# Three waiting projection matmuls placed between the four transposes of an attention output

## The chip, the cores and the metric

One core of one Trainium2 chip runs the kernel. The time is device microseconds from one launch to its end. TensorE is PE in the profile (its weight loads are PEld), VectorE is DVE, ScalarE is ACT, GpSimd is POOL, and SyncE, which issues the DMAs, is SP.

## The reference

The kernel computes one encoder layer on 1024 tokens of width 1024 with two kinds of attention side by side.

```
h = x @ w_in                                   # (1024, 3328): q_a k_a v_a z_a q_b k_b v_b z_b
y_a = neighborhood_attention(q_a, k_a, v_a, rel_bias)     # 8 heads, window 8 x 16 on a 16 x 64 grid
y_b = windowed_gqa_with_sink(rotary(q_b), rotary(k_b), v_b, sink)   # 8 heads, 2 of k and v, |i-j| <= 128
mixed = concatenate([y_a * silu(z_a), y_b * silu(z_b)])
y = mixed @ w_out
x = layer_norm(alpha * x + y, gain, bias)
```

## The kernel before

The matrix products run as split products: a value is kept as a high and a low part, and three products (high by high, high by low, low by high) are summed in a PSUM bank.

**Projection.** `project(name)` is a generator. It makes 128 columns of `h` in two halves of 512 tokens. Each half is a *group* of 24 matmuls (L356, 512 columns wide, half precision) that sum into one bank. The generator gives control back after each matmul, so its matmuls can be dealt out one by one. There are two banks of this kind, tag `pj` (`ps_pj` in the profile), and `new_group` hands them out in turn. When a group is complete, `evac` empties its bank. For a group of q or k, ACT writes the high part (L235) and DVE the low part (L241), for each of two heads: four operations, dealt out over the following steps. For a gate it is a Tanh on ACT (L319) and a product on DVE (L320). The first matmul of a new group has to wait until the bank, last used two groups before, has been emptied.

**Attention.** The work is cut into 128 units (a block of 128 queries of one head): 64 of group B, then 64 of group A. The main loop makes a step per unit. In a step it emits the scores of one unit (`stage_qk`: two matmuls L709 and L710 on PE, and a sum with minimum on DVE, L719), the Exp on ACT (L735, `stage_exp`), and for the unit before it the split of the probabilities (`stage_tr`: ACT L745, DVE L746) and their transposition by a DMA (L749). Four units make a *quad*. Once in four steps `stage_pv` emits the quad's product of probabilities and values (L774: 33 or 36 small matmuls, 64 columns each), and `stage_on` scales the result on DVE (L783). Every other quad has both heads of a pair ready. Then `stage_ot`, which comes ahead of `stage_pv` in the step, transposes the pair's output on PE: four 128 by 128 transposes in float32 (L794) into one bank of tag `t`, from where DVE multiplies them into the gate (L797 for group B, twice L803 for group A).

**What sets the order.** The main loop runs under a hand-written order: each engine gets its instructions as the program emits them. `fill` is the list of generators that wait to give matmuls: the projections that are not done yet, then the first part of the output projection (L899, `out_head`, float32 operands). `pump(n)` takes `n` matmuls from it. A table says how many are due by each point of the loop. `pump_to` takes as many as are missing, and `pumped` counts what has been given, so matmuls that were taken early are missing from the next portions:

```
    def pump_to(u):
        ...
        pump(n - pumped[0])
        pumped[0] = max(n, pumped[0])
```

In a step the order on PE is: `stage_qk`, `stage_ot`, `stage_pv`, a small portion (`pump_to(i + F1)`), and at the end of the step the rest (`pump_to(i + 1)`), some six matmuls in all. After the loop, `final` does the rest of the output projection and the layer norm; its order is made by a scheduler.

Of the kernel before, what the change touches and what calls it, by code (L numbers as in the profile page):

```python
# [55 lines left out]
def hybrid_block(ctx, tc, xT, x, wt, wv, wo, bias, sink, gain, lbias, cos, sin, bmask, out):  # L56
# [11 lines left out]
    def bank(tag):  # L68
        bufs = {"pj": 2, "s": 4, "t": 2}[tag]
        return (ps1 if bufs == 1 else ps2).tile([128, 512], F32, tag=tag, name=f"ps_{tag}", bufs=bufs)  # L70
# [87 lines left out]
    def need(*ops):  # L158
        for op in ops:
            if op.step is None:  # L160
                need(*op.deps)
                queues[op.eng].remove(op)
                op.emit()
# [161 lines left out]
    def z_col(e):  # L325
        return vsc if e in (4, 0, 5) else vscb[:, 0:1] if e == 1 else vscb[:, 1:2]
# [45 lines left out]
    def pump(n):  # L372
        while n > 0 and fill:
            try:
                next(fill[0])
                n -= 1
            except StopIteration:
                fill.pop(0)
# [373 lines left out]
    def quad(q):  # L752
        g, p, j, t, _ = units[4 * q]
        return g, p, j, t // 4 if g == "b" else t[0] // 2
# [31 lines left out]
    def stage_ot(q):  # L786
        g, p, j, h = quad(q)
        if j == 0:
            return
        need(*stk_ops.get(f"zb{p}" if g == "b" else f"z{p}", ()))  # L790
        ps = bank("t")
        o = on.pop((g, p, h))
        for i in range(4):
            nc.tensor.transpose(ps[:, 128 * i:128 * i + 128], o[:, i].rearrange("p h e -> p (h e)"), identf)  # L794
        if g == "b":
            z = zt[4 + p][:, 512 * h:512 * h + 512]
            nc.vector.scalar_tensor_tensor(z, ps, z_col(4 + p), z, op0=ALU.mult, op1=ALU.mult)  # L797
        else:
            for i in range(2):
                b = 2 * h + i  # L800
                z = zt[p].rearrange("p (r c) -> p r c", c=GW)[:, :, 16 * b:16 * b + 16]
                src = ps[:, 256 * i:256 * i + 256].rearrange("p (r c) -> p r c", c=16)
                nc.vector.scalar_tensor_tensor(z, src, z_col(p), z, op0=ALU.mult, op1=ALU.mult)  # L803
# [6 lines left out]
    pumped = [0]  # L810
# [227 lines left out]
    for i in range(-LD, NU + LO):  # L1038
# [34 lines left out]
        if m == 0 and 0 <= q - 1 < NU // 4:  # L1073
            stage_ot(q - 1)
# [97 lines left out]
```

## Time and profile before

| | |
|---|---|
| time, median of three runs | 458.9 us |
| the three runs | 458.0, 458.9, 458.96 us |
| span of the profiled execution, first to last instruction | 457.0 us |
| time of the profiled execution beside its span | not given apart; the median of the runs lies 1.9 us above the span |
| PE busy | 445.1 us, 97% |
| DVE, ACT, POOL busy | 333.6, 287.8, 228.4 us |
| L356, 512 columns wide | 1008 matmuls |
| L794, transposes | 64 |

The span is read as stretches: a prologue, the main loop, in which projection matmuls fill what attention leaves free on PE, and from about 377 us the output projection and the norm. Records of matmuls overlap, since one starts while the one before still drains. So the time that a matmul costs PE is read from the distance between starts, and a hole on PE is a start that comes later than the form of the matmul before it explains.

### The profile page before, as it was taken

What the parts mean: (1) busy time and instruction counts of PE and PEld (TensorE: products, weight loads), DVE (VectorE), ACT (ScalarE), POOL (GpSimd) and SP (SyncE); (2) the same over time, 40 slices, a digit from 0 to 9 for tenths busy, and PEclk for the clock granted to TensorE, in tenths of its full rate; (3) what the DMA queues carried; (4) which work ended last, traced back from release to release, by engine and by line L of the source; (5) the groups of instructions that cost most, each with busy time, mean ns of one, the idle gap of its engine ahead of it and who ended that gap; (6) DMA issues with size and microseconds to landing.
All of it is one profiled execution on the core that took longest, in us unless ns stands there. A gap on an engine that the chain in (4) does not pass through costs nothing.

```text
span 457.0 us, 9394 instructions
## 1 busy us (share of the span) xinstructions
PE 445.1 (97%) x3238; PEld 295.3 (65%) x3238; DVE 333.6 (73%) x808; ACT 287.8 (63%) x664; POOL 228.4 (50%) x236
## 2 busy tenths in 40 slices
PE   7999999999999999999999999999999999999993
PEld 5999984444445555555555656555556788888882
DVE  4884967608988787797888887877868739099644
ACT  4627838878478878787868887786878824012100
POOL 1001953574948658688416766544663445007621
PEclk9999999999999999999999999999999999999997
DMA  7895457986658698598978979889989877004511
GB/s 222 304 309 219 139 191 270 263 300 224 227 89 182 134 190 141 127 157 151 173 130 186 177 162 224 156 191 207 191 192 225 166 224 295 0 14 149 187 58 54
DMA packets 134319, 82.28 MB, mean 180 GB/s; under 512 B 101344, under 2 KB 113376, under 8 KB 134016
## 3 DMA queue, kind: packets, MB, share of 16 engines
q1 hardware_dynamic: 133936, 81.26, 72.2%
q8 instruction: 25, 0.41, 0.4%
q0 software_dynamic: 48, 0.16, 0.2%
q10 hardware_dynamic: 288, 0.26, 0.2%
q14 instruction: 22, 0.18, 0.1%
HBM read 51.25 MB, written 9.96 MB: 134 GB/s over the span
## 4 chain that ended last, share of the span: by engine, by line
PE 91%; DVE 3%; issue 2%; ACT 2%; DMA 1%; DVEq 0%; POOL 0%; POOLq 0%; ACTq 0%
PE ps_pj L356 44%; PE ps_s L899 9%; PE ps_t L774 6%; PE ps_s L430 6%; PE ps_pj L899 6%; PE ps_t L899 5%; PE ps_s L709 4%; PE ps_s L710 4%; PE ps_pj L430 3%; PE ps_t L430 3%; PE ps_t L794 1%; DMA wvraw<-in_wv 1%; DVE qs L241 1%; ACT split L745 1%; DVE split L746 1%
## 5 line engine op out<-in xcount | busy, mean ns | idle before, releaser
L356 PE MATMUL ps_pj<-xf,wh 128*128 128x512 f16 x672 | 202.2, 379 | 0.9 <-DVE qs L241 0.6
L356 PE MATMUL ps_pj<-xf,wl 128*128 128x512 f16 x336 | 127.3, 379 | 0.0
L356 PEld LDWEIGHTS <-wh 128*128 128x128 f16 x672 | 63.5, 98 | 61.6 <-DVE ks L241 1.0
L735 ACT ACTIVATE ps_s<-sn,nm 128x385 f32<-128x385 f32 (+3 forms) x128 | 70.3, 549 | 33.0 <-DVE nm L719 31.8
L746 DVE SCALAR_TENSOR_TENSOR split<-ps_s,split 128x384 f16<-128x384 f32 (+2 forms) x128 | 65.6, 513 | 27.5 <-ACT split L745 26.1
L745 ACT ACTIVATE split<-ps_s 128x384 f16<-128x384 f32 (+2 forms) x128 | 57.4, 449 | 1.8
L356 PEld LDWEIGHTS <-wl 128*128 128x128 f16 x336 | 32.9, 98 | 37.4
L719 DVE CUSTOM_DVE_ANT_0 sn<-ps_s,bm,nsk 128x384 f32<-128x384 f32 (+1 forms) x64 | 40.8, 638 | 6.9 <-PE ps_s L710 6.4
L899 PE MATMUL ps_s<-wo,m 128*128 128x512 f32 (+1 forms) x192 | 43.3, 379 | 0.0
L719 DVE CUSTOM_DVE_ANT_0 sn<-ps_s,bias,sg 128x264 f32<-128x264 f32 (+1 forms) x64 | 35.0, 547 | 10.9 <-PE ps_s L710 4.7
L187 POOL TENSOR_SCALAR wr<-wr,wsc 128x512 f32<-128x512 f32 x26 | 20.6, 793 | 39.9 <-ACT wh L182 33.8
L709 PE MATMUL ps_s<-ks,qs 128*128 128x384 f16 (+4 forms) x128 | 39.3, 307 | 0.0
L710 PE MATMUL ps_s<-ks,qs 128*128 128x384 f16 (+4 forms) x128 | 39.2, 306 | 0.0
L899 PEld LDWEIGHTS ps_s<-wo,m 128*128 128x128 f32 x192 | 34.4, 188 | 7.0
L681 POOL TENSOR_SCALAR bias<-bias,rsg 128x552 f32<-128x552 f32 (+1 forms) x24 | 19.2, 799 | 38.0 <-DMA bias<-in_bias 34.5
L774 PEld LDWEIGHTS <-tr 128*128 128x128 f16 (+1 forms) x1104 | 36.5, 98 | 2.2 <-issue 0.3
L953 ACT ACTIVATE sd<-mv,eps 128x1 f32<-128x1 f32 x8 | 2.4, 296 | 50.5 <-DVE mv L951 46.5
L188 POOL TENSOR_TENSOR wl<-wr,wh 128x512 f16<-128x512 f32 x26 | 32.6, 1255 | 2.2
L273 POOL COPY ks<-ks 64x512 f16<-64x512 f16 x40 | 26.3, 665 | 10.3 <-DVE ks L241 5.4
L430 PE MATMUL ps_s<-wvh,x 128*128 128x320 f32 x128 | 30.8, 320 | 0.0
L989 POOL TENSOR_TENSOR xr<-xr,gb 128x512 f32<-128x512 f32 x7 | 10.3, 1475 | 40.8 <-ACT xr L986 40.8
L899 PE MATMUL ps_pj<-wo,m 128*128 128x512 f32 (+1 forms) x120 | 28.6, 376 | 0.0
(148 smaller groups left out, 830.0 us busy)
## 6 DMA issues: line engine op xcount, KB each, us to landing
xraw<-in_xT SPq DMA_DIRECT2D x31, 256.0 KB, 4.2
ws<-in_wt SPq DMA_DIRECT2D x15, 512.0 KB, 5.6
wr<-in_wt SPq DMA_DIRECT2D x26, 256.0 KB, 3.2
bias<-in_bias SPq DMA_DIRECT2D x16, 276.0 KB, 3.4
wor<-in_wo SPq DMA_DIRECT2D x16, 256.0 KB, 3.5
xr<-in_x SPq DMA_DIRECT2D x8, 512.0 KB, 7.3
out<-xr SPq DMA_DIRECT2D x14, 256.0 KB, 2.0
bias<-in_bias SPq DMA_DIRECT2D x8, 368.0 KB, 4.4
```

The lines of the kernel that those rows point to most:

```text
L188: nc.gpsimd.tensor_sub(l, raw, h)
L273: nc.gpsimd.tensor_copy(t[o, sl], t[a, sl])
L356: nc.tensor.matmul(ps, a[:, k % 4, :], mv, start=(k == 0 and i == 0), stop=(k == KT - 1 and i == 2))
L430: nc.tensor.matmul(ps[:, :320], lh[t // 4, k][:, ts], rh[k][:, cs], start=(k == 0 and i == 0), stop=(k == KT - 1 and i == 2))
L709: nc.tensor.matmul(ps[:, :m], q, sl[0], start=True, stop=False)
L710: nc.tensor.matmul(ps[:, :m], q, sl[1], start=False, stop=True)
L719: nc.vector.tensor_tensor_reduce(sn[:, :m], ps[:, :m], bias_t, sg[:, c:c + 1], init, op0=ALU.add, op1=ALU.min, accum_out=nm)
L735: nc.scalar.activation(pt[:, :m], sn[:, :m], AF.Exp, bias=nm, scale=-1.0, accum_out=sm[:, k:k + 1])
L745: nc.scalar.activation(hl[:, :m, 0, :c], src, AF.Copy, scale=PSCALE)
L746: nc.vector.scalar_tensor_tensor(hl[:, :m, 1, :c], src, PSCALE, hl[:, :m, 0, :c], op0=ALU.mult, op1=ALU.subtract)
L774: nc.tensor.matmul(ps[:, HD * m:HD * m + HD], a, b_, start=(i == 0), stop=(i == len(mms) - 1))
L899: nc.tensor.matmul(ps, lh[:, ts], rh[:, cs], start=(e == EO[0] and i == 0), stop=(e == EO[-1] and i == 2))
```

## The change

After each of the first three transposes one matmul is taken from `fill`, and counted as given. The portions that follow in the step are smaller by three.

```
         for i in range(4):
             nc.tensor.transpose(ps[:, 128 * i:128 * i + 128], o[:, i].rearrange("p h e -> p (h e)"), identf)
+            if i < 3:
+                pump(1)
+                pumped[0] += 1
         if g == "b":
```

## The prediction

> **What bounds the kernel now.** I read the page first, then a table of stages, then the waits of PE, then single rows of the timeline around the transposes.
>
> ```profile
> span 457.0 us, 9394 instructions
> PE 445.1 (97%) x3238; PEld 295.3 (65%) x3238; DVE 333.6 (73%) x808; ACT 287.8 (63%) x664; POOL 228.4 (50%) x236
> ...
> PEclk9999999999999999999999999999999999999997
> ...
> PE 91%; DVE 3%; issue 2%; ACT 2%; DMA 1%; DVEq 0%; POOL 0%; POOLq 0%; ACTq 0%
> ```
>
> PE is busy 97% of the span, carries 91% of the chain that ended last, and its granted clock is full in all slices but the last. The table of stages says the same of the stretch that the change touches:
>
> ```profile
> core 0: us, PE busy (x) PEld busy (x) DVE busy (x) ACT busy (x) POOL busy (x), PEclk, DMA share, GB/s
> 162.00:194.00 32.00, 32.00 (x292) 18.64 (x291) 24.01 (x70) 24.44 (x62) 22.32 (x24) 1.00 0.81 151
> 194.00:248.00 54.00, 53.66 (x496) 30.84 (x493) 44.73 (x126) 42.66 (x110) 31.02 (x33) 1.00 0.86 158
> ...
> 377.00:449.00 72.00, 72.00 (x338) 59.65 (x336) 47.31 (x85) 13.19 (x24) 25.34 (x18) 1.00 0.31 113
> ```
>
> PE has no hole from 162 to 194 and from 377 to 449, so a microsecond by which PE comes later in between is still there at the end. PE's waits after the prologue are only these two, and both are for the same thing, a projection bank (`ps_pj`) that DVE (L241) has not yet emptied:
>
> ```profile
> PE ps_pj L356 <- DVE qs L241: 0.6, 1, 0.6
> ...
> PE ps_pj L356 <- DVE ks L241: 0.3, 1, 0.3
> ```
>
> So PE is bound by its own stream, and the only thing that stops it here is the rotation of the two `ps_pj` banks. A change in PE's order has two possible effects: a different cost per instruction, or a wait that comes at another moment.
>
> **The change part by part: what moves.** The listing of both programs' instructions, engine by engine, shows that DVE, ACT, POOL and SP keep their order exactly. On PE the order changes at 15 of the 16 places with transposes: 13 times three projection matmuls (L356), twice three of the output projection (L899); at the last nothing is waiting. The three stood behind the 33 or 36 P·V matmuls (L774) that follow the transposes, and now stand between the transposes. Nothing is added or dropped, and by the next score matmuls (L709) PE has done the same work. Rows of one place, PE and then DVE (start, duration, line):
>
> ```profile
> 193.01 0.33 PE L710 MATMUL ps_s<-ks,qs 128*128 128x384 f16 x1
> 193.17 0.60 PE L794 MATMUL ps_t<-identf,on 128*128 128x128 f32 x4
> 193.61 1.13 PE L774 MATMUL ps_t<-vb,tr 128*128 128x64 f16 x33
> 194.57 0.60 PE L356 MATMUL ps_pj<-xf,wh 128*128 128x512 f16 x2
> 195.00 0.38 PE L356 MATMUL ps_pj<-xf,wl 128*128 128x512 f16 x1
> ...
> 193.56 0.69 DVE L241 SCALAR_TENSOR_TENSOR ks<-ps_pj,ks 64x512 f16<-64x512 f32 x1
> ```
>
> **Cost per instruction: nothing.** Durations in these rows overlap, so starts are compared. Two L356 take 195.00 - 194.57 = 0.43 us, 0.216 each. Four transposes take 193.61 - 193.17 = 0.44, 0.11 each. A transpose between two wide matmuls exists already, at L558:
>
> ```profile
> 68.39 0.38 PE L356 MATMUL ps_pj<-xf,wh 128*128 128x512 f16 x1
> 68.61 0.27 PE L558 MATMUL ps_s<-identf,vg 128*128 128x128 f32 x1
> 68.72 0.38 PE L356 MATMUL ps_pj<-xf,wh 128*128 128x512 f16 x1
> ```
>
> The wide matmul ahead of it takes 0.22, the transpose 0.11: the same in both neighbourhoods, to 10 ns. So 39 moved L356 and their transposes cost 0.
>
> A rule says otherwise, and it speaks for a gain: the Trainium skill, "TensorE: Matmul & The Clock Gate", sections "LDWEIGHTS" and "Weight-path perf modes", puts a load of 128 columns at 128/1.2 = 107 ns and denies FP32 weights the fast load, so the 0.11 would be the next transpose's weight load, which a wide matmul ahead hides; with the 56 ns that its section "Back-to-back issue gap" gives for 128 columns, 45 times 53 ns, 2.4 us, would be saved. The L558 rows speak against it: the load ahead of that transpose had a wide matmul to hide behind, a half-precision load followed, and it still took 0.11.
>
> The six L899, read here in the same way:
>
> ```profile
> 354.29 0.94 PE L899 MATMUL ps_pj<-wo,m 128*128 128x512 f32 x3
> 355.08 0.32 PE L709 MATMUL ps_s<-ks,qs 128*128 128x352 f16 x1
> ```
>
> Three behind P·V take 0.79, 0.26 each. Between transposes no row shows them; the nearest bounds are 0.22 (a wide L356, 0.04 less) and 0.31 (0.05 more). Six times that is -0.24 to +0.30; I take 0, since half-precision neighbours change nothing at L558.
>
> **The wait that moves.** The first moved matmul is often the first of a new group, and it waits for its bank. It now comes 0.11 after the first transpose's start instead of after P·V. In the rows above: due at 193.17 + 0.11 = 193.28 instead of 194.57, 1.29 earlier. DVE empties the bank at 193.56 + 0.69 = 194.25. Before, that was 0.3 ahead of PE; now it is 1.0 behind. PE takes things in order, so the transposes 2 to 4, P·V and the next scores queue up behind the waiting matmul. The rows of a stall that exists give the wake-up, and the size of a hole that is worth remembering:
>
> ```profile
> 247.20 0.31 PE L710 MATMUL ps_s<-ks,qs 128*128 128x352 f16 x1
> 247.86 0.60 PE L356 MATMUL ps_pj<-xf,wh 128*128 128x512 f16 x2 [0.34 <-DVE ks L241]
> ...
> 247.10 0.69 DVE L241 SCALAR_TENSOR_TENSOR ks<-ps_pj,ks 64x512 f16<-64x512 f32 x1
> ```
>
> DVE ends at 247.79 and PE starts at 247.86: 0.07 to wake. So the new stall at 193 is 194.25 + 0.07 - 193.28 = 1.04. DVE will not be earlier: from 181.5 to 194.2 it waits once for PE, and otherwise goes back and forth with ACT:
>
> ```profile
> DVE split L746 <- ACT split L745: 2.6, 4, 0.7
> DVE sn L719 <- PE ps_s L710: 0.5, 1, 0.5
> ```
>
> The same subtraction at the other places where DVE's L241 frees the bank near the transposes (in the rest it is free before the first transpose starts):
>
> ```profile
> 231.06 0.60 PE L794 MATMUL ps_t<-identf,on 128*128 128x128 f32 x4
> 230.79 0.69 DVE L241 SCALAR_TENSOR_TENSOR qs<-ps_pj,qs 64x512 f16<-64x512 f32 x1
> ...
> 284.09 0.60 PE L794 MATMUL ps_t<-identf,on 128*128 128x128 f32 x4
> 283.41 0.69 DVE L241 SCALAR_TENSOR_TENSOR ks<-ps_pj,ks 64x512 f16<-64x512 f32 x1
> ...
> 291.70 0.60 PE L794 MATMUL ps_t<-identf,on 128*128 128x128 f32 x4
> 291.33 0.69 DVE L241 SCALAR_TENSOR_TENSOR qs<-ps_pj,qs 64x512 f16<-64x512 f32 x1
> ...
> 321.88 0.60 PE L794 MATMUL ps_t<-identf,on 128*128 128x128 f32 x4
> 321.26 0.69 DVE L241 SCALAR_TENSOR_TENSOR ks<-ps_pj,ks 64x512 f16<-64x512 f32 x1
> ```
>
> At 231: 231.48 + 0.07 - 231.17 = 0.38. At 284: 284.17 against 284.20, none, with 0.03 to spare. At 291: 292.09 - 291.81 = 0.28. At 321: 322.02 - 321.99 = 0.03.
>
> **What is given back.** A stall is kept unless a later wait of PE shrinks by it. The matmul of 247.86 was due at 247.35 (L710 takes 0.16 for 384 columns at 193.01, so 0.15 for 352): that stall holds 0.51. The L241 that ends it closes a run of DVE and ACT work that PE sets going at 226.6; from 226.7 to 247.1 DVE waits for PE only at that very start:
>
> ```profile
> DVE sn L719 <- PE ps_s L710: 0.2, 1, 0.2
> ```
>
> So the stall of 247 absorbs the one at 231, unless that one delays DVE too, and it does:
>
> ```profile
> 233.70 0.33 PE L710 MATMUL ps_s<-ks,qs 128*128 128x384 f16 x1
> 234.15 0.67 DVE L719 CUSTOM_DVE_ANT_0 sn<-ps_s,bm,nsk 128x384 f32<-128x384 f32 x1
> ```
>
> These scores end at 234.03, only 0.12 before DVE takes them. 0.38 later makes DVE 0.26 late. Whether the 13 us of DVE and ACT work that follow pass this on can't be read from a row: PE keeps between 0 and 0.38 of this stall. Since DVE is busy or waiting for ACT all the way, I take it that all is passed on: PE gets 0.12 back, and 0.26 stays. The stall at 193 lies before 226.6, so DVE moves with PE, and nothing is given back.
>
> Sum: 1.04 + 0.26 + 0.28 + 0.03 = 1.6 us. The span goes from 457.0 to 458.6; the median of the runs is 1.9 above the span, so the time goes from 458.9 to 460.5. Unknown besides the L899: at 193 and at 284 the wait sits on the weight load, not on the matmul, which adds between 0 and 0.11 (a transpose's interval) each.
>
> **What else comes later.** DVE's multiplication by the gate (L797, L803) waits for the fourth transpose, which ends three wide matmuls later. The tightest place is the L899 one at 352:
>
> ```profile
> 353.45 0.87 DVE L803 SCALAR_TENSOR_TENSOR z<-ps_t,vscb,z 128x256 f32<-128x256 f32 x2
> 354.47 0.46 DVE L746 SCALAR_TENSOR_TENSOR split<-ps_s,split 128x288 f16<-128x288 f32 x1
> 355.68 0.58 DVE L719 CUSTOM_DVE_ANT_0 sn<-ps_s,bias,sg 128x352 f32<-128x352 f32 x1 [0.76 <-PE ps_s L710]
> ```
>
> It would start up to 3 x 0.22 = 0.65 later. Behind it on DVE is L746; 355.68 has 0.76 of idle ahead, which hides it. I cost it at nothing; without that cover it is 0.65 here.
>
> **The rivals.**
> *No change.* The bank at 193 is free before 193.28 in most executions, because DVE and ACT run about 1 us less far behind PE there than in the one profiled; 459.5 where only this stall goes, 458.9 where the other releases come that much earlier too. For it: the three times spread by 0.96 us, as much as this term. Against it: the run of DVE and ACT since 181.5 has fixed lengths and little waiting on PE. It decides at 194.25: where L241 ends 0.7 earlier, the sum falls to 0.9. Chance 0.2.
> *Faster.* What a transpose takes is the wait for its weights, which the wide matmul now covers. Its own streaming would be 128 columns at L356's 0.216 for 512, 0.054; 45 times 0.056 is 2.5 us less. PE then reaches the banks no later, so the 1.6 of stalls stays: 458.0. L558 speaks against it. Chance 0.06. (It is the case of the rule of the Trainium skill above, from "TensorE: Matmul & The Clock Gate".)
> *Slower than forecast.* DVE's late gate multiplications are not covered and come back at PE as later bank releases: 0.65 at three places like 353, some 2 us: 462.5. Against it: the 0.76 of idle. Chance 0.1.
> That the change doesn't do what it says is ruled out by the listing.
>
> **How the numbers follow.** A measurement of this kernel can tell about 0.2% (0.9 us) from no change. Forecast, chance 0.64: 460.5, with 460.0 to 461.1 as its own range (less 0.24 and 0.26, or more 0.30, 0.22 and 0.12, for L899, the weight loads and what 247 gives back). The range 458.8 to 461.8 takes in most of the no-change case and part of the slower one. Faster 0.05 (that case, less a little). Same 0.21: 0.17 of the no-change case, 0.01 of faster, 0.03 of the forecast with small stalls. Slower 0.74, the rest.
>
> **What would show it.** In the profile after: a hole on PE at 193.4 of about 1 us, between the first and the second transpose, put down to DVE ks L241; one of 0.4 at 232 and one of 0.3 near 293; the hole of 0.51 at 247.86 about 0.1 smaller; the transposes' intervals at 0.11 beside the L356's 0.216. Wrong would be: transposes at 0.05, or no hole at 193, or a PE that finishes L774 at the old times.

## The result: 2.0 us slower, and the holes are where the banks turn over

| | before | after |
|---|---|---|
| time, median of 7 runs | 457.96 us (456.22 to 458.96) | 459.96 us (458.86 to 460.36) |
| span of the profiled execution | 457.0 us | 458.6 us |
| time of the profiled execution of after | | 460.36 us |

The ratio is 1.0044, with an interval of 1.0023 to 1.0065. A later series of the same two kernels gave 1.0031 (1.0013 to 1.0050). Both hold the forecast's 1.6 us, 1.0035.

The page of after, the lines that answer to those of before:

```profile
span 458.6 us, 9394 instructions
PE 446.0 (97%) x3238; PEld 296.5 (65%) x3238; DVE 334.2 (73%) x808; ACT 287.9 (63%) x664; POOL 228.1 (50%) x236
...
PEclk9999999999999999999999999999999999999998
...
PE 85%; DVE 4%; issue 3%; ACT 2%; DMA 2%; POOL 2%; DVEq 0%; POOLq 0%; ACTq 0%
```

The number of instructions, the granted clock and, within a few tenths of a microsecond, the work of the other engines are the same. PE's share of the chain that ended last fell from 91 to 85%: the chain now leaves PE at its new waits. PE's waits in after (who waited for whom, total us, times, longest):

```profile
PE ps_pj L356 <- DVE ks L241: 0.9, 1, 0.9
PE ps_pj L356 <- DVE qs L241: 0.8, 2, 0.6
...
PE ps_t L774 <- DMA tr<-split: 0.4, 1, 0.4
```

The view counts idle time after the modelled end of the last matmul, so it shows less than the starts do. The first new wait, in PE's rows of the timeline and the DVE row that ends it:

```profile
192.53 0.27 PE L794 MATMUL ps_t<-identf,on 128*128 128x128 f32 x1
193.66 0.39 PE L356 MATMUL ps_pj<-xf,wh 128*128 128x512 f16 x1 [0.86 <-DVE ks L241]
193.89 0.27 PE L794 MATMUL ps_t<-identf,on 128*128 128x128 f32 x1
194.00 0.38 PE L356 MATMUL ps_pj<-xf,wh 128*128 128x512 f16 x1
194.22 0.27 PE L794 MATMUL ps_t<-identf,on 128*128 128x128 f32 x1
...
192.91 0.69 DVE L241 SCALAR_TENSOR_TENSOR ks<-ps_pj,ks 64x512 f16<-64x512 f32 x1
```

The first transpose starts at 192.53, and the moved matmul, due at 192.64, starts at 193.66, just after DVE has freed its bank at 193.60: a hole of 1.02. From there on a transpose takes 0.11 (193.89 to 194.00) and a wide matmul 0.22 (194.00 to 194.22), as in before. The same reading at the other places of after:

```profile
231.45 0.27 PE L794 MATMUL ps_t<-identf,on 128*128 128x128 f32 x1
231.93 0.38 PE L356 MATMUL ps_pj<-xf,wh 128*128 128x512 f16 x1 [0.21 <-DVE qs L241]
...
247.96 0.31 PE L710 MATMUL ps_s<-ks,qs 128*128 128x352 f16 x1
248.41 0.60 PE L356 MATMUL ps_pj<-xf,wh 128*128 128x512 f16 x2
...
292.25 0.27 PE L794 MATMUL ps_t<-identf,on 128*128 128x128 f32 x1
292.64 0.38 PE L356 MATMUL ps_pj<-xf,wh 128*128 128x512 f16 x1
```

Holes of 0.37 at 231 and 0.28 at 292, and the one at 248 is 0.30 (due at 248.11) where it was 0.51. At 322 it is 0.02 (transpose at 322.71, matmul at 322.84), and at 284 there is none. The sum on PE is 1.02 + 0.37 - 0.21 + 0.28 + 0.02 = 1.48.

Two profiles of one kernel differ by more than that in the prologue, so the main loop is measured by itself: from the first to the last score matmul on PE. The row of L709 gives both (duration, first and last start). Before it was 127.6 to 361.9, 234.3 us; after:

```profile
L709 PE MATMUL ps_s<-ks,qs x128: 272/324/337, 126.9 to 363.5; 128*128 128x384 f16 x64, 128*128 128x256 f16 x16, 128*128 128x264 f16 x16, 128*128 128x288 f16 x16
```

236.6 us. To a hundredth, by the starts in the timeline, it is 234.36 in before (127.55 to 361.91) and 236.56 in after (126.91 to 363.47), 2.2 more. 1.5 of it are the bank waits. Another 0.8 was not forecast: P·V waits for transposed probabilities near 360 us. (The moved output-projection matmuls at 353 give back 0.09; see below.)

```profile
359.68 1.21 PE L774 MATMUL ps_t<-va,tr 128*128 128x64 f16 x27
361.25 0.44 PE L774 MATMUL ps_t<-va,tr 96*128 96x64 f16 x9 [0.36 <-DMA tr<-split]
```

36 of these matmuls took 1.05 in before, at 353.24 (to the L899 at 354.29) as at this place (358.91 to the L899 at 359.96); here they take 1.84, from 359.68 to the next L902 at 361.52. (L902 is the L899 of before; the change adds three lines above it.)

### The profile page after: what moved, and what is told of

Its sections match the earlier page's. It is cut to its first block, busy times and chain, and to the rows that moved or that the text cites. A ratio compares the mean times of both kernels' runs of the same rounds, so it can differ in the third digit from the quotient of the medians.

```text
span 458.6 us, 9394 instructions
## 1 busy us (share of the span) xinstructions
PE 446.0 (97%) x3238; PEld 296.5 (65%) x3238; DVE 334.2 (73%) x808; ACT 287.9 (63%) x664; POOL 228.1 (50%) x236
## 4 chain that ended last, share of the span: by engine, by line
PE 85%; DVE 4%; issue 3%; ACT 2%; DMA 2%; POOL 2%; DVEq 0%; POOLq 0%; ACTq 0%
PE ps_pj L356 40%; PE ps_s L902 9%; PE ps_s L430 6%; PE ps_t L774 6%; PE ps_pj L902 5%; PE ps_t L902 5%; PE ps_pj L430 3%; PE ps_s L709 3%; PE ps_s L710 3%; PE ps_t L430 3%; PE ps_t L794 1%; DVE ks L241 1%; ACT split L745 1%; DMA wvraw<-in_wv 1%; DVE split L746 1%
## 5 line engine op out<-in xcount | busy, mean ns | idle before, releaser
L746 DVE SCALAR_TENSOR_TENSOR split<-ps_s,split 128x384 f16<-128x384 f32 (+2 forms) x128 | 65.7, 513 | 26.4 <-ACT split L745 25.2
L902 PE MATMUL ps_s<-wo,m 128*128 128x512 f32 (+1 forms) x192 | 43.7, 380 | 0.0
L709 PE MATMUL ps_s<-ks,qs 128*128 128x384 f16 (+4 forms) x128 | 39.3, 307 | 0.0
L902 PEld LDWEIGHTS ps_s<-wo,m 128*128 128x128 f32 x192 | 34.4, 188 | 7.1
L902 PE MATMUL ps_pj<-wo,m 128*128 128x512 f32 (+1 forms) x120 | 28.9, 378 | 0.0
```

The source lines that it names most:

```text
L709: nc.tensor.matmul(ps[:, :m], q, sl[0], start=True, stop=False)
L746: nc.vector.scalar_tensor_tensor(hl[:, :m, 1, :c], src, PSCALE, hl[:, :m, 0, :c], op0=ALU.mult, op1=ALU.subtract)
L902: nc.tensor.matmul(ps, lh[:, ts], rh[:, cs], start=(e == EO[0] and i == 0), stop=(e == EO[-1] and i == 2))
```

## The experiments

All were timed in several rounds beside before. Where the loop is given, it is the time from the first to the last score, to be held against 234.3 of before.

**The change again.** The kernel is the changed one.

> The changed kernel once more. If the waits of P.V near 360 us (0.25 and 0.52 us, for DMA transpositions) belong to the change, they come again; if they are the DMA queue's own variation from run to run, they differ or are gone while the holes at 193, 231 and 291 come again to within 0.05 us. Time +1.5 to +2.3 us against before.

Measured: ratio 1.0031 (1.0013 to 1.0050). The loop runs from 128.5 to 364.3, 235.8 us, 1.4 more than before (235.78 against 234.36). The holes come again, 1.02 at 194, 0.37 at 233, 0.27 at 294, and 0.30 instead of 0.51 near 250. The wait of P·V does not:

```profile
361.26 1.22 PE L774 MATMUL ps_t<-va,tr 128*128 128x64 f16 x36
362.31 0.94 PE L902 MATMUL ps_pj<-wo,m 128*128 128x512 f32 x3
```

36 matmuls, no hole, 1.05 to the next start. So the 0.8 us near 360 do not come with every execution of the change, while the bank waits do, to 0.01 us. They account for the 1.4: 1.48, less 0.07 at the output projection's place near 354.

**The late places alone, and all but them.** At five places DVE's L241 frees the new group's bank close to the transposes.

```
-            if i < 3:
+            if i < 3 and q not in (6, 11, 18, 19, 23):     # skip_late; "q in (...)" in only_late
                 pump(1)
                 pumped[0] += 1
```

> The interleaving as in the change, but at 10 of its 15 places: the five where DVE frees the bank late (the ones near 193, 231, 284, 291 and 321 us) keep the old order. Theory (the time went into bank waits at those places): PE shows no hole of over 0.1 us between transposes, the L356 and transposes beside each other still take 0.216 and 0.11, the holes at 247 and 337 are 0.5 and 0.7 as before, and the time is that of before, within 0.3 us (ratio 0.999 to 1.001). Rival (alternating float32 transposes and half-precision matmuls costs, or the later gate multiplications delay the DMA transpositions that P.V waits for, as at 360 us after the change): two thirds of the 2.0 us stay, +1.3 us, and P.V waits some 0.8 us near 360.

> The complement: only the five places where DVE frees the bank late have the interleaving. Theory: holes of 1.03 at 193, 0.37 at 231 and 0.28 at 291, 0.2 given back at 247, so +1.5 us against before (ratio 1.003). Rival (the alternation or the DMA transpositions): a third of the 2.0 us, +0.7 us.

Measured: without the late places the ratio is 0.9999 (0.9983 to 1.0015) and the loop 234.3 (126.1 to 360.4). With them alone it is 1.0030 (1.0015 to 1.0044), and the loop 235.9 (125.8 to 361.7). PE's waits on the banks without the late places are those of before:

```profile
PE ps_pj L356 <- DVE qs L241: 0.6, 1, 0.6
PE ps_pj L356 <- DVE ks L241: 0.3, 1, 0.3
```

With the late places alone the hole at 191 is that of after:

```profile
191.46 0.27 PE L794 MATMUL ps_t<-identf,on 128*128 128x128 f32 x1
192.59 0.39 PE L356 MATMUL ps_pj<-xf,wh 128*128 128x512 f16 x1 [0.85 <-DVE ks L241]
```

So ten places with interleaving cost nothing, and the five cost all (the one at 284 has no hole even so). Single places say the same: the stretch from the first transpose to the next scores at 201 us takes 2.69 in before (200.84 to 203.53) and 2.70 in after (201.23 to 203.93). Alternating transposes with matmuls of the projection is free.

**The same three matmuls behind the fourth transpose.**

```
             nc.tensor.transpose(ps[:, 128 * i:128 * i + 128], o[:, i].rearrange("p h e -> p (h e)"), identf)
-            if i < 3:
-                pump(1)
-                pumped[0] += 1
+            if i == 3:
+                pump(3)
+                pumped[0] += 3
```

> The same three matmuls at all 15 places, but in one block behind the fourth transpose, ahead of P.V, so that nothing alternates. The moved matmul is due 0.44 us after the first transpose instead of 0.11. Theory: the holes shrink by 0.33 each: 0.70 at 193, 0.04 at 231, none at 291 and 321; +0.7 us against before (ratio 1.0015). Rival (alternation costs): no loss, ratio 1.000. Rival (later gate multiplications: the fourth transpose is no later here): no wait of P.V near 360.

Measured: ratio 1.0010 (0.9995 to 1.0025), which by the clock can't be told from none; the loop is 235.0 (127.0 to 362.0), 0.7 more than before.

```profile
192.62 0.60 PE L794 MATMUL ps_t<-identf,on 128*128 128x128 f32 x4
193.76 0.60 PE L356 MATMUL ps_pj<-xf,wh 128*128 128x512 f16 x2 [0.54 <-DVE ks L241]
```

Due at 192.62 + 0.44 = 193.06, started at 193.76: a hole of 0.70, as forecast, with nothing alternating. At 231 it is the 0.04 of the forecast. The hole depends on when the group's first matmul comes up, not on what stands beside it.

**Three banks for the groups**, one of them taken from the scores, in before's order and in the change's. (One bank of the prologue and one part of the output projection, `out_head((2,), ...)`, go over to the tag `pj` with it; these lines are left out here.)

```
-        bufs = {"pj": 2, "s": 4, "t": 2}[tag]
+        bufs = {"pj": 3, "s": 3, "t": 2}[tag]
...
-            if len(groups) >= 2:
-                need(*groups[-2])
+            if len(groups) >= 3:
+                need(*groups[-3])
```

> The order of before (no interleaving), with three banks for the projection groups and three instead of four for the scores, so that a new group needs the bank of three groups ago. Theory (PE's holes are the rotation of two banks): the holes of 0.51 near 247 and 0.72 near 337 are gone, -1.2 us against before (ratio 0.997), if the scores never wait for their three banks. Rival (the holes are DVE and ACT running behind, whatever the banks): they come back as waits of the scores L709 for a bank, no gain or a loss.

> The changed kernel with the same three banks. Theory: no hole between transposes at 193, 231 and 291, and the time is that of before with three banks, within 0.2 us: 3.2 us less than the changed kernel would be at ratio 1.0035, so ratio 0.997 against before. Rival (alternation costs by itself): still 1 us or more above before with three banks.

Measured: 1.0024 (1.0008 to 1.0040) in before's order and 1.0018 (1.0006 to 1.0030) in the change's. The interleaving costs nothing here: the loops are 235.9 (127.8 to 363.7, with 0.47 us of P·V waiting for a DMA in it) and 235.3 (126.5 to 361.8). The changed kernel's PE at the place of the largest hole, and its waits:

```profile
192.49 0.32 PE L709 MATMUL ps_s<-ks,qs 128*128 128x384 f16 x1 [0.57 <-DVE split L746]
192.65 0.32 PE L710 MATMUL ps_s<-ks,qs 128*128 128x384 f16 x1
192.81 0.27 PE L794 MATMUL ps_t<-identf,on 128*128 128x128 f32 x1
192.92 0.38 PE L356 MATMUL ps_pj<-xf,wh 128*128 128x512 f16 x1
...
PE ps_s L709 <- DVE split L746: 0.8, 2, 0.6
PE ps_s L709 <- DVE sn L714: 0.3, 1, 0.3
PE ps_s L709 <- DVE qs L241: 0.2, 1, 0.2
```

The hole between the transposes is gone, and so are the two holes that before has at 247 and 337. The scores now wait for DVE instead, in both orders alike, and the hoped-for 1.2 us of gain turned into a loss of about 1. The theory held for what the change costs; for the holes that before has, the rival held: here PE meets DVE's lateness at the score banks.

**Evacuations dealt out twice as fast.**

```
-        pop("dve", ND if i < M_AT[1] else 2)
+        pop("dve", 2)
...
-        pop("act", NA if i < M_AT[0] and len(queues["act"]) < 5 else 2)
+        pop("act", 2)
```

> The order of before, but in each step of the main loop two waiting operations are dealt to ACT and two to DVE instead of one, so a group's four evacuations take fewer steps. Theory: L241 frees the banks some 1 to 3 us earlier, the holes near 247 and 337 go or shrink, up to -1.2 us. Rival: ACT and DVE do the evacuations ahead of the Exp and the splits, the attention's own chain comes late, and PE waits for scores or transposed probabilities instead: +0 to +3 us.

> The changed kernel with the same two operations dealt per step. Theory: the bank at 193 is free by the time the first transpose is done, the holes of the change (1.03, 0.37, 0.28) shrink to under 0.3 together, and the time is that of before with two per step, within 0.3 us. Rival: the holes stay, +1.5 us against it.

Measured: before's order 1.0036 (1.0021 to 1.0050), the change's 1.0028 (1.0012 to 1.0044). The largest hole falls from 1.02 to 0.14 (192.01 to 192.25, where 0.11 is the transpose), because its bank is freed earlier:

```profile
192.01 0.27 PE L794 MATMUL ps_t<-identf,on 128*128 128x128 f32 x1
192.25 0.39 PE L356 MATMUL ps_pj<-xf,wh 128*128 128x512 f16 x1
...
190.80 1.40 DVE L241 SCALAR_TENSOR_TENSOR ks<-ps_pj,ks 64x512 f16<-64x512 f32 x2
```

DVE is done with it at 192.20, 0.19 after the first transpose's start, where in after that was 1.07.

The other two hardly move: 0.34 and 0.27. So the forecast of under 0.3 together failed, with 0.75. The loops are 235.8 (125.0 to 360.8) and 236.2 (126.4 to 362.6), a difference of 0.4 for the interleaving. By the clock the two orders don't differ, and both lose against before. Of the holes of before's order, the one near 337 shrinks (0.72 to 0.35), but the one near 247 grows (0.51 to 0.75), and in both orders PE waits once 1.16 us, as the rival said, for q that DVE splits too late for its scores. In before's order:

```profile
337.39 0.30 PE L709 MATMUL ps_s<-ks,qs 128*128 128x288 f16 x1 [1.16 <-DVE qs L241]
```

**The opposite move.** Before's order, with the next scores ahead of a new group's first six matmuls in one step.

```
+        if clock["step"] == 66:
+            n = min(n, -(-pumped[0] // 24) * 24)
         pump(n - pumped[0])
```

> The opposite of the change at one place of the kernel before: in step 66 (near 247 us), where PE waits 0.51 us for DVE to free the new group's bank, the group's first six matmuls are held back behind the next unit's scores (two matmuls of 0.15 us each). Theory (what counts is when a new group's first matmul comes up in PE's order): the hole shrinks by the 0.30 of the two score matmuls, to about 0.2, and the main loop from the first to the last score is 0.3 us shorter than before's 234.3; by the clock that is ratio 0.9993, too small to be told from none. Rival (the hole is DVE's lateness, which catches PE elsewhere): a wait of the same size appears at another matmul and the main loop stays at 234.3.

Measured: ratio 0.9994 (0.9978 to 1.0011), none that can be told. The loop is 234.1 (127.1 to 361.2), and the hole:

```profile
246.93 0.33 PE L709 MATMUL ps_s<-ks,qs 128*128 128x384 f16 x1
247.10 0.33 PE L710 MATMUL ps_s<-ks,qs 128*128 128x384 f16 x1
247.46 0.61 PE L356 MATMUL ps_pj<-xf,wh 128*128 128x512 f16 x2
```

Due at 247.26, started at 247.46: 0.20 instead of 0.51, and no other wait grew. To a hundredth the loop is 234.07 (127.13 to 361.20) where it was 234.36: the 0.3 of the forecast, so the rival, a wait of the same size elsewhere, did not hold here. The timing of whole runs does not resolve it. No other version here has a loop that is shorter by more than 0.04, and none measurably beats before.

## Why the prediction was right, step by step

- *Cost per instruction, nothing.* Right: 0.11 and 0.22 in after, and no loss at ten places. By the prediction's estimate from the rule of the Trainium skill ("TensorE: Matmul & The Clock Gate", "LDWEIGHTS" and "Weight-path perf modes") the transposes would have fallen to half behind a wide matmul; the trace disagrees, 193.89 to 194.00 is 0.11.
- *The L899, taken as 0.* Right to 0.1. At the place of 352 a transpose and its L902 take 0.34 together (rows below), where 0.11 and 0.26 were counted. From the first transpose to the next scores that is 2.19 (353.66 to 355.85) instead of 2.28 (352.80 to 355.08), 0.09 less; at the second such place, near 370, it is 0.04 more over the same instructions. How the 0.34 divides can't be read: the starts give the transpose 0.03 and the L902 0.32.

```profile
353.66 0.27 PE L794 MATMUL ps_t<-identf,on 128*128 128x128 f32 x1
353.69 0.48 PE L902 MATMUL ps_pj<-wo,m 128*128 128x512 f32 x1
354.01 0.27 PE L794 MATMUL ps_t<-identf,on 128*128 128x128 f32 x1
```

- *The moved wait.* Right in place and size: 1.04, 0.38, none, 0.28 and 0.03 forecast, and 1.02, 0.37, none, 0.28 and 0.02 found. That the wait sits on the weight load at 193 and at 284 cost nothing. The rival of no change, a bank at 193 that is free early in most executions, did not hold: the hole is 1.02 in all three profiles that have the interleaving there with before's banks and evacuations (after, its repetition, and the late places alone).
- *What is given back.* Right in kind, a little off in size: 0.12 was forecast, 0.21 measured. The step that failed is "I take it that all is passed on". DVE took the scores late as forecast, but lost part of the lateness on its way to L241 at 247. The rows of after:

```profile
234.82 0.68 DVE L719 CUSTOM_DVE_ANT_0 sn<-ps_s,bm,nsk 128x384 f32<-128x384 f32 x1 [0.19 <-PE ps_s L710]
...
235.42 0.55 DVE L746 SCALAR_TENSOR_TENSOR split<-ps_s,split 128x384 f16<-128x384 f32 x1
...
247.66 0.69 DVE L241 SCALAR_TENSOR_TENSOR ks<-ps_pj,ks 64x512 f16<-64x512 f32 x1
```

  From the first to the last it took 12.84, and 12.95 before (234.15 to 247.10). All of the difference lies in the first step: in before the L746 behind these scores started 0.72 after them, here 0.60.

```profile
234.87 0.56 DVE L746 SCALAR_TENSOR_TENSOR split<-ps_s,split 128x384 f16<-128x384 f32 x1
```

  From L746 to L241 it is 12.23 before and 12.24 here. So DVE had 0.12 of slack in this one place, which the view of waits does not list, and the 12 us behind it passed everything on.
- *The late gate multiplication.* Right: in after it waits for the transposes, and the next scores on DVE still have idle time ahead of them, so it reaches no bank.

```profile
355.00 0.88 DVE L806 SCALAR_TENSOR_TENSOR z<-ps_t,vscb,z 128x256 f32<-128x256 f32 x2 [0.61 <-PE ps_t L794]
...
356.45 0.58 DVE L719 CUSTOM_DVE_ANT_0 sn<-ps_s,bias,sg 128x352 f32<-128x352 f32 x1 [0.21 <-issue]
```

- *The agreement of the span, 458.6 forecast and found, is partly luck.* The loop lost 2.2, with 0.8 of a DMA wait that nothing in the forecast has, and the prologue of that execution was 0.6 shorter. The loop of the second execution, 1.4 more, is the better proof. The level of the time, 460.5, came out 0.5 above the measured 459.96, because it was counted from the 458.9 of three runs, and seven runs of before have a median of 457.96.

Open: why P·V waited near 360 in one execution of the change and not in the other. A wait of this kind also appeared in the kernel with three banks in before's order (0.47 us), so it needs no interleaving; whether a later PE makes it likelier was not tried.

## What to carry to other kernels

Moving work earlier on a full engine is free only if what the work waits for is ready by its new time. Before moving a matmul, take from the trace when its bank, its weights and its input become ready, subtract the new due time, and sum what is positive; here that gave each hole to 0.02 us, while what the matmuls themselves cost changed by less than 0.1. Then look for the next stall of the same engine, since it may give part of it back.

## What the runs showed of the hardware that was not expected

The prologue, whose work is the same in all these kernels but for the names of its banks, differs between executions by more than the change is worth: the first score starts between 125.0 and 128.5 us in the eleven profiles here, while the loop behind it repeats its holes to 0.01 us. All of that spread arises in the first 30 us or so: from the 150th matmul to the first score it takes 97.83 to 97.85 us in every profile. Two things differ there. One is a wait of PE for weights that arrive by DMA (ACT's first use of them, L414): 0.5 us in after, 1.3 in before, 2.1 in the changed kernel's second profile. The other is how long PE's matmuls go at a slower pace. In before:

```profile
10.97 0.47 PE L430 MATMUL ps_s<-wvl,x 128*128 128x320 f32 x1
11.23 0.45 PE L430 MATMUL ps_pj<-wvl,x 128*128 128x320 f32 x1
...
11.67 0.31 PE L430 MATMUL ps_t<-wvl,x 128*128 128x320 f32 x1
11.81 0.31 PE L430 MATMUL ps_s<-wvl,x 128*128 128x320 f32 x1
```

Up to 11.50 such a matmul takes 0.27 from start to start, from 11.67 on 0.15. 18 of them take 0.27 in before, 22 in the changed kernel's second profile, whose first score is the last of all (128.5), and 2 in the profile of before's order with two evacuations per step, whose first score is the earliest (125.0). At 0.12 each, the 20 between those two make 2.4 of their 3.5 us. The PEclk row of the page has a 9 in that slice all the same. What sets the moment of the step was not tried. The single runs of before, 455.8 to 459.8 us, spread by about as much as the first scores do. Differences of a microsecond are therefore read from the loop of a profile, or from many runs.

A transposing DMA takes the issuing queue 1.21 us, and now and then over twice that: the same transposition in before and in after.

```profile
348.81 1.21 SPq L749 DMA_TRANSPOSE tr<-split  x1
```

```profile
349.93 2.84 SPq L749 DMA_TRANSPOSE tr<-split  x1
```

Behind it the queue issues row on row, about 0.1 us apart, and the transpositions that P·V waited for near 360 are issued at 356.75 and 358.06 (354.81 and 356.12 in before), 1.9 later, while PE is only 0.8 later at that P·V. The second profile of the change has such a long one too, 2.72 for the next transposition, with no wait on PE behind it.
